# A float32 decoder block on one core: where the first feed-forward's early steps are formed, and in which order its entry runs

## The chip, the cores and the metric

The kernel runs on one core of one Trainium2 chip. The metric is the device time of one execution in microseconds (us); lower is better. The engines are named as in the profile: PE is TensorE (PEld its weight loads), DVE is VectorE, ACT is ScalarE, POOL is GpSimd, SP is SyncE, which only issues DMAs here. "L504" is line 504 of the kernel before.

## The reference, cut to what matters

One layer on 512 tokens of width 1024, all in float32:

```python
h = h + 0.5 * swiglu(rmsnorm(h, ffn1_norm[i]), ffn1_w_gate[i], ffn1_w_up[i], ffn1_w_down[i])
n = rmsnorm(h, mix_norm[i])
...                                     # token mixing: spatial gating beside a state-space part
h = h + jnp.concatenate([ya, yb], axis=-1) @ w_out[i]
h = h + 0.5 * swiglu(rmsnorm(h, ffn2_norm[i]), ffn2_w_gate[i], ffn2_w_up[i], ffn2_w_down[i])
gate = jax.nn.sigmoid(rmsnorm(h, ple_norm[i]) @ ple_w_gate[i] + ple_b_gate[i])
h = h + gate * (p[i] @ ple_w_proj[i])
return rmsnorm(h, final_norm)
```

`p` has 256 features a token. `p @ ple_w_proj`, the embedding product, is used last but depends on nothing else.

## The kernel before, in words

**Precision.** Each float32 operand is split in two: a high part (a cast by ACT, tiles `whi`, `ghi`, `xfa`, `xfb`) and a low part (operand minus high part, mostly by DVE, tiles `wlo`, `glo`, and the second halves of `xfa` and `xfb`). A product is three matmul passes: high by high, high weight by low input, low weight by high input. A weight block is 128x1024 floats (512 KB); its cast is L500, its low part L504.

**The entry.** TensorE first runs ten matmuls on zeros (L181). Then comes the embedding product, in two steps (`embedding(q)`, q = 0 and 1) of four output blocks with 24 matmuls each, since it needs only `p` (256 KB for each half of its features, tile `g`) and a weight block `raw<-in_ple_proj`. Its results wait in DRAM (`emb_dram`) until the end of the kernel; they are copied out of PSUM by L1007 into tiles `embt`, `p7`, `u2` and `rawd`, and stored from there by L967.

Behind it stand four steps on the first group of the first feed-forward (24 matmuls of 512 columns each): gate and up on the first half of the input blocks (`xfa`), then gate and up on the second half (`xfb`). They are plain products. From the second group on the kernel uses a scheme with seven products in place of eight (24 matmuls of 256 columns each, L709), whose inputs are the blocks themselves and their sums and differences. Product number 5 of the scheme takes as its input the difference of the token halves of the first input blocks: `Early.t1` forms it at L614, ScalarE casts it at L617, and GpSimd forms the low part at L620. The differences lie in a tile that takes turns with `embt` in one buffer. The other differences are formed at L648 and L650, cast at L631, their low parts at L634.

The norm's factor is not applied to the inputs but to the products: `RowNorm` sums the squares of the input rows (L361, in the tiles `whix`, `wlox`, `g` and `s1`, which later hold other things), DVE computes the factor with small operations (L233 to L238), spreads it on a diagonal (L297 to L301, tile `tmp`), and two matmuls (L314) on PE bring it to all partitions. They stand on PE between the last of the four plain steps and the first product of the scheme. Scheme product 3 needs a weight block plus another: GpSimd issues a DMA (L761) that adds the second onto the first in `rawb`. Likewise L724 and L727 for other blocks.

**What sets the order.** On PE, ACT, DVE and SP the order of the instructions is the order in which the program writes them. `run` makes a task of each step's load, split, product and after-work, cut into pieces at each `yield`; the table `ENTRY` says which task goes on by how many pieces at the start, and what it doesn't list follows in the loop's own order. GpSimd's queue follows from the program too.

Of the kernel before, what the change touches and what calls it, by code (L numbers as in the profile page):

```python
# [25 lines left out]
F32 = mybir.dt.float32  # L26
# [3 lines left out]
ALU = mybir.AluOpType  # L30

P = 128
T = 512
NC = T // P
D = 1024
ND = D // P
# [4 lines left out]
HT = T // 2  # L41
# [6 lines left out]
LOADS, MIX_LOADS = 6, 4  # L48

ENTRY = """  # L50
load0 load1 load1.1 load2 load3 load3.1 load4 load5 split0 split1:1 split1.1:2 split1 split1.1
load6 load6.1 product0 split2 split3.1:3 split3.1:1 load7 product1 after0 split3:1 split4.1:1
split3 split4.1:1 split3.1:1 split4.1:2 split3.1:1 split4.1:1 split3.1 split4.1 load8 product2
after1:1 after1 split4 split5.1:1 split4.2:2 split5:1 split4.2:2 split5 split5.1:1 split4.2
load9 product3 split5.1 split5.2 split6.2:1 split5.3 product4 split6 split6.1 split6.2:1
split6.2 product5 after4 after4.1 split7 split7.1 load12 product6 split8 after5 product7 sums9
split10.1:1 after6 split9 load14 product8 after7 split10 split10.1 load15 split14:1 product9
split11 after8 load16 split14 product10 after9 split12:1 after10 split12 load17 product11
after11 split13 split15:1 after10.1 split15 product12 split16:1 after12:1 after+10 after11.1
after11.2 product13 split16 after+11 after12 product14 after13:1 sums18 after13 load21 product15  # L60
split17
"""

BUFS = {
# [26 lines left out]
_COL = {}  # L91
# [8 lines left out]
def layer_kernel(ctx: ExitStack, tc: tile.TileContext, a: dict, out: bass.AP):  # L100
    nc = tc.nc
# [44 lines left out]
    def acc_ps():  # L146
        turns["acc"] += 1
        return bank(f"a{turns['acc'] % 2}", 1)
# [6 lines left out]
    def sm_ps():  # L155
        return bank("sm", 3)
# [3 lines left out]


    vec = sb("vec", (P, NVEC))
    nc.scalar.dma_start(vec, a["vecs"])

    def col(name, i):
        c = _COL[name] + i
# [12 lines left out]
    ps = sm_ps()  # L179
# [399 lines left out]
    class Early:  # L579
# [28 lines left out]
        @staticmethod  # L608
        def t1(both):

            f = sb("embt", (P, 2, 2, HT))
            for n, e in enumerate(both):
                x11, x12 = (e.hg[0].rearrange("p k (s t) -> p s k t", s=2)[:, s] for s in range(2))
                nc.vector.tensor_tensor(f[:, n], x11, x12, ALU.subtract)  # L614
                yield
            for n, e in enumerate(both):
                nc.scalar.copy(e.a[:, 1, 0], f[:, n])  # L617
                yield
            for n, e in enumerate(both):
                nc.gpsimd.tensor_tensor(e.a[:, 1, 1], f[:, n], e.a[:, 1, 0].bitcast(F32), ALU.subtract)  # L620
                yield

        @staticmethod
# [34 lines left out]
    def former(name, xfs):  # L658

        neg = sb(f"neg{name}", (P, ND))  # L660
        nc.vector.tensor_scalar(neg, vec[:, _COL[name] : _COL[name] + ND], -1.0, None, ALU.mult)

        def done(d):
            c = (col(name, d), neg[:, d : d + 1])
            if d < NP:
                XForms(xfs).first(h[d], c)
            else:
                xfs[d - NP].second(h[d], c)
        return done
# [293 lines left out]
    pe, stores = [], []  # L963

    def store_embedding():
        for to, t in stores:
            nc.sync.dma_start(to, t)  # L967

    def embedding(q):
        w = Parts()  # L970
        ps = []
        raw = sb("g", (P, 2, T)) if q == 0 else None

        def load():
            if q:
                w.load(a["ple_proj"][q])
                return
            nc.sync.dma_start(raw[:, 0], a["p"][:, 0])
            w.load(a["ple_proj"][q])
            nc.sync.dma_start(raw[:, 1], a["p"][:, 1])  # L980

        def split():
            if q:
# [11 lines left out]

        def product():

            for i in range(4):
                ps.append(acc_ps() if i == 3 else bank("mm", 3) if q else sm_ps())
                accumulate(ps[i], (w.hi, w.lo), 2 * i, pe)  # L1000

        def out():
            for i, tag in enumerate(("embt", "embt", "p7", "u2", "rawd", "rawd", "rawd", "rawd")[4 * q : 4 * q + 4]):
# [47 lines left out]
    ffn1_steps = steps  # L1051
# [95 lines left out]
    for name in ORDER:  # L1147
        kind, i = name[0], int(name[1]) if name != "dt" else 0
# [235 lines left out]
    n = at["x4"] + 1  # L1384
# [82 lines left out]
    n = at["z0"]  # L1467
    for j in range(ND):
        n = at[f"z{j}"]
# [5 lines left out]
    n = at["z0"] + 2  # L1475
# [100 lines left out]
    n = at["v7"]  # L1576
# [7 lines left out]
    for j in range(ND):  # L1584
        n = at[f"z{j}"]
# [220 lines left out]
def _laid_out(i):  # L1806
# [88 lines left out]
```

## Time and profile before

| | before |
|---|---|
| median of 3 runs | 1083.53 us (1083.05 to 1084.03) |
| the profiled execution | 1082.95 us, span 1081.2 us |
| PE, DVE, ACT, POOL busy | 1069.3, 780.3, 515.6, 139.4 us |
| granted TensorE clock, mean | 0.998 |
| DMA moved | 163.77 MB, mean 151 GB/s |

The span is the time from the first to the last instruction; 1.75 us of the profiled execution lie around it. TensorE is busy for 99% of the span, so a change can gain only what TensorE waits for, and most of that lies in the first 43 us and in the last few. In the rows of the timeline the columns are start, duration, engine, line, operation, tiles, shape, and in brackets the idle time before it with what ended it. A busy matmul's duration overlaps the next one's; the pace is the distance between starts.

### The profile page before, as it was taken

How to read it: one execution, taken by the hardware profiler on the slowest of the kernel's cores; microseconds unless marked ns; L12 is line 12 of the kernel's file. 1: busy time of each engine (PE TensorE's matmuls, PEld its weight loads, DVE VectorE, ACT ScalarE, POOL GpSimd, SP SyncE). 2: the span in 40 equal slices, each digit the busy share in tenths (PEclk: the TensorE clock that was granted, in tenths of full speed). 3: DMA queues.
4: the chain of work that ended last, by engine and by line, in shares of the span. 5: the costliest groups of instructions: out<-in, count | busy, mean ns of one | idle time of the engine just before them, and what ended most of it. 6: DMA issues, size and time to landing. Idle time of an engine off the chain costs nothing.

```text
span 1081.2 us, 16536 instructions
## 1 busy us (share of the span) xinstructions
PE 1069.3 (99%) x6679; PEld 946.3 (88%) x6679; DVE 780.3 (72%) x1078; ACT 515.6 (48%) x711; POOL 139.4 (13%) x127
## 2 busy tenths in 40 slices
PE   9999999999999999999999999999999999999997
PEld 7899999999998788787878888899999999999886
DVE  7887776766666686766997656778766676667766
ACT  7644343434444455575654434354444444343554
POOL 0200000000000300143233000000000000000411
PEclk9999999999999999999999999999999999999999
DMA  9987766575523332444332333667756676633412
GB/s 362 274 223 195 196 177 190 150 193 169 137 59 117 98 98 81 137 137 137 125 109 79 98 98 98 214 160 201 220 140 161 190 193 178 177 116 106 145 42 79
DMA packets 49741, 163.77 MB, mean 151 GB/s; under 512 B 5632, under 2 KB 5888, under 8 KB 49664
## 3 DMA queue, kind: packets, MB, share of 16 engines
q1 hardware_dynamic: 39584, 128.99, 35.1%
q0 software_dynamic: 8640, 31.46, 16.9%
q10 hardware_dynamic: 1440, 2.26, 0.7%
q8 instruction: 52, 0.85, 0.3%
q14 instruction: 25, 0.20, 0.1%
HBM read 158.43 MB, written 4.26 MB: 150 GB/s over the span
## 4 chain that ended last, share of the span: by engine, by line
PE 88%; DVE 6%; DMA 3%; ACT 2%; issue 1%; DVEq 0%; SPq 0%; ACTq 0%
PE mm L709 20%; PE a L709 15%; PE sm L216 10%; PE sm L215 10%; PE sm L217 10%; PE mm L216 4%; PE mm L215 4%; PE mm L217 4%; PE a L215 3%; PE a L217 3%; PE a L216 3%; DMA emb_dram<-embt 1%; DVE wlo L504 1%; DMA whix<-in_x_rows 1%; DMA raw<-in_ffn_gu 1%
## 5 line engine op out<-in xcount | busy, mean ns | idle before, releaser
L500 ACT CAST whi<-raw 128x1024 fp32r<-128x1024 f32 x138 | 144.3, 1046 | 159.8 <-issue 56.8
L504 DVE TENSOR_TENSOR wlo<-raw,whi 128x1024 fp32r<-128x1024 f32 x137 | 171.9, 1255 | 61.6 <-ACT whi L500 60.0
L709 PE MATMUL mm<-xfb,whi 128*128 128x256 f32 x960 | 166.0, 276 | 0.0
L709 PEld LDWEIGHTS mm<-xfb,whi 128*128 128x128 f32 x960 | 145.8, 188 | 1.6
L709 PE MATMUL mm<-xfb,wlo 128*128 128x256 f32 x480 | 132.6, 276 | 0.0
L217 PE MATMUL sm<-ghi,wlox 128*128 128x512 f32 x296 | 116.3, 393 | 0.0
L216 PE MATMUL sm<-glo,whix 128*128 128x512 f32 x296 | 115.9, 391 | 0.0
L215 PE MATMUL sm<-ghi,whix 128*128 128x512 f32 x296 | 115.1, 389 | 0.0
L709 PE MATMUL a<-xfb,whi 128*128 128x256 f32 x640 | 110.9, 276 | 0.0
L709 PEld LDWEIGHTS a<-xfb,whi 128*128 128x128 f32 x640 | 97.8, 188 | 1.9 <-issue 0.2
L709 PEld LDWEIGHTS mm<-xfb,wlo 128*128 128x128 f32 x480 | 90.1, 188 | 0.0
L709 PE MATMUL a<-xfb,wlo 128*128 128x256 f32 x320 | 88.4, 276 | 0.4 <-DVE wlo L504 0.4
L504 DVE TENSOR_TENSOR wlox<-rawd,whix 128x1024 fp32r<-128x1024 f32 (+1 forms) x40 | 45.6, 1141 | 58.8 <-ACT whix L500 58.8
L504 DVE TENSOR_TENSOR wlo<-rawb,whi 128x1024 fp32r<-128x1024 f32 x52 | 64.7, 1244 | 19.9 <-ACT whi L500 19.8
L852 ACT ACTIVATE g<-g 128x512 f32<-128x512 f32 x40 | 25.3, 632 | 106.3 <-DVE g L850 106.3
L724 POOL DMA_DIRECT2D raw<-in_ffn_gu x20 | 17.3, 865 | 404.1 <-DMA raw<-in_ffn_gu 120.9
L908 DVE SCALAR_TENSOR_TENSOR h<-sm,h 128x512 f32<-128x512 f32 x96 | 63.2, 683 | 6.4 <-PE sm L217 5.8
L500 ACT CAST whi<-rawb 128x1024 fp32r<-128x1024 f32 x52 | 54.3, 1044 | 28.4 <-DVE rawb L719 17.7
L217 PEld LDWEIGHTS sm<-ghi,wlox 128*128 128x128 f32 x296 | 55.5, 188 | 11.7
L215 PEld LDWEIGHTS sm<-ghi,whix 128*128 128x128 f32 x296 | 55.6, 188 | 10.8
L216 PEld LDWEIGHTS sm<-glo,whix 128*128 128x128 f32 x296 | 55.5, 188 | 10.8
L709 PEld LDWEIGHTS a<-xfb,wlo 128*128 128x128 f32 x320 | 60.1, 188 | 0.6 <-DVE wlo L504 0.6
(417 smaller groups left out, 2497.1 us busy)
## 6 DMA issues: line engine op xcount, KB each, us to landing
raw<-in_ffn_gu SPq DMA_DIRECT2D x56, 512.0 KB, 5.9
rawd<-in_ffn_down SPq DMA_DIRECT2D x40, 512.0 KB, 4.0
rawb<-in_ffn_gu SPq DMA_DIRECT2D x32, 512.0 KB, 5.3
raw<-in_ffn_gu POOLq DMA_DIRECT2D x30, 512.0 KB, 5.6
raw<-in_w_in SPq DMA_DIRECT2D x29, 512.0 KB, 3.6
s<-in_ffn_gu SPq DMA_DIRECT2D x20, 512.0 KB, 6.8
s<-in_ffn_gu POOLq DMA_DIRECT2D x20, 512.0 KB, 8.3
raw<-in_w_out SPq DMA_DIRECT2D x16, 512.0 KB, 3.6
```

Of the source, the lines that this page charges most:

```text
L215: nc.tensor.matmul(ps, whi, xhi, start=first, stop=False)
L216: nc.tensor.matmul(ps, whi, xlo, start=False, stop=False)
L217: nc.tensor.matmul(ps, wlo, xhi, start=False, stop=last)
L500: nc.scalar.copy(self.hi[:, : self.n], self.raw[:, : self.n])
L504: nc.vector.tensor_tensor(self.lo[:, :n], self.raw[:, :n], self.hi[:, :n].bitcast(F32), ALU.subtract)
L709: nc.tensor.matmul(o, wt[:, c], xt, start=fresh and p == m == n == 0, stop=last and n == 2, skip_group_check=True,)
L724: nc.gpsimd.dma_start(w21.raw, self.src[0], accum_op=ALU.add)
L852: nc.scalar.activation(t, t, AF.Silu)
L908: nc.vector.scalar_tensor_tensor(h[d], ps[d], 0.5, h[d], ALU.mult, ALU.add)
```

## The change

Five edits.

1. The embedding product goes by input block: for each half of `p`'s features all four output banks take high by high, then high weight by low input, then low weight by high input. The host lays the weight out to match, so that the first half of the input features has the first half of the columns, and the weight of step q = 0 is loaded in two DMAs of 256 KB.
2. The vector of norm gains (`vec`) is loaded by SP, behind these loads, and no longer by ACT's queue.
3. `Early.t1` puts its differences in the buffer `whix`, and its low parts are formed by VectorE.
4. The negated gains of the second feed-forward (`neg`) are formed in the last step of the first feed-forward.
5. The table `ENTRY` is written anew. `store_embedding` empties its list as it goes; it issues the same five stores.

```diff
 ENTRY = """
-load0 load1 load1.1 load2 load3 load3.1 load4 load5 split0 split1:1 split1.1:2 split1 split1.1
...
+load0 load1 load1.1 load2 load3 load3.1 split0 load4 split1:1 load5 split1.1:2 split1 split1.1
...
     vec = sb("vec", (P, NVEC))
-    nc.scalar.dma_start(vec, a["vecs"])
...
         def t1(both):
 
-            f = sb("embt", (P, 2, 2, HT))
+            f = sb("whix", (P, 2, 2, HT))
...
             for n, e in enumerate(both):
-                nc.gpsimd.tensor_tensor(e.a[:, 1, 1], f[:, n], e.a[:, 1, 0].bitcast(F32), ALU.subtract)
+                nc.vector.tensor_tensor(e.a[:, 1, 1], f[:, n], e.a[:, 1, 0].bitcast(F32), ALU.subtract)
                 yield
...
         neg = sb(f"neg{name}", (P, ND))
-        nc.vector.tensor_scalar(neg, vec[:, _COL[name] : _COL[name] + ND], -1.0, None, ALU.mult)
+        also(
+            ffn1_steps[-1], "split",
+            lambda: nc.vector.tensor_scalar(
+                neg, vec[:, _COL[name] : _COL[name] + ND], -1.0, None, ALU.mult
+            ),
+        )
...
     def store_embedding():
-        for to, t in stores:
-            nc.sync.dma_start(to, t)
+        while stores:
+            nc.sync.dma_start(*stores.pop(0))
...
             nc.sync.dma_start(raw[:, 0], a["p"][:, 0])
-            w.load(a["ple_proj"][q])
+            w.raw = sb(w.tag, (P, 1024))
+            for k in range(2):
+                c = slice(k * T, (k + 1) * T)
+                nc.sync.dma_start(w.raw[:, c], a["ple_proj"][q][:, c])
             nc.sync.dma_start(raw[:, 1], a["p"][:, 1])
+            nc.sync.dma_start(vec, a["vecs"])
...
         def product():
 
-            for i in range(4):
-                ps.append(acc_ps() if i == 3 else bank("mm", 3) if q else sm_ps())
-                accumulate(ps[i], (w.hi, w.lo), 2 * i, pe)
+            ps.extend(acc_ps() if i == 3 else bank("mm", 3) if q else sm_ps() for i in range(4))
+            for k, (xhi, xlo) in enumerate(pe):
+                for n, (wt, xt) in enumerate(((w.hi, xhi), (w.hi, xlo), (w.lo, xhi))):
+                    for i in range(4):
+                        c = slice((4 * k + i) * P, (4 * k + i + 1) * P)
+                        nc.tensor.matmul(ps[i], wt[:, c], xt, start=k == n == 0, stop=k == 1 and n == 2)
...
-    o["ple_proj"] = np.ascontiguousarray(pj.transpose(0, 2, 1, 3).reshape(2, P, 8 * P))
+    o["ple_proj"] = np.ascontiguousarray(
+        pj.reshape(2, 4, P, 2, P).transpose(0, 2, 3, 1, 4).reshape(2, P, 8 * P)
+    )
```

What this does to the queues, at three places.

On PE, before, the first step of the embedding product finishes one bank after the other (`sm_188`, `sm_195`, ... are PSUM banks; `ghi`, `glo` are the parts of `p`, `whi`, `wlo` those of the weight):

```order
L215 MATMUL sm_188<-ghi_152,whi_154 128x512
L216 MATMUL sm_188<-glo_153,whi_154 128x512
L217 MATMUL sm_188<-ghi_152,wlo_155 128x512
L215 MATMUL sm_195<-ghi_152,whi_154 128x512
L216 MATMUL sm_195<-glo_153,whi_154 128x512
L217 MATMUL sm_195<-ghi_152,wlo_155 128x512
```

Now it begins with twelve matmuls on the first input half, four banks in turn for each kind of part:

```order
L1010 MATMUL sm_188<-ghi_148,whi_150 128x512
L1010 MATMUL sm_189<-ghi_148,whi_150 128x512
L1010 MATMUL sm_190<-ghi_148,whi_150 128x512
L1010 MATMUL a_59_191<-ghi_148,whi_150 128x512
L1010 MATMUL sm_188<-glo_149,whi_150 128x512
L1010 MATMUL sm_189<-glo_149,whi_150 128x512
L1010 MATMUL sm_190<-glo_149,whi_150 128x512
L1010 MATMUL a_59_191<-glo_149,whi_150 128x512
L1010 MATMUL sm_188<-ghi_148,wlo_151 128x512
L1010 MATMUL sm_189<-ghi_148,wlo_151 128x512
L1010 MATMUL sm_190<-ghi_148,wlo_151 128x512
L1010 MATMUL a_59_191<-ghi_148,wlo_151 128x512
```

The parts of the second input half are first read by the thirteenth matmul, where before they were read by the fourth. The rest of PE's order, up to the end of the kernel, is as before.

On DVE, before, the two differences of `Early.t1` (`embt_370`) stand on both sides of the low parts for scheme products 4 (`xfb`) and 1 (`wlo_401`), ahead of the norm's small operations (`nv`, ...):

```order
L650 SCALAR_TENSOR_TENSOR glo_275<-glo_223,glo_275 128x512
L614 TENSOR_TENSOR embt_370<-ghi_167 128x512
L634 TENSOR_TENSOR xfb_110<-ghi_272,xfb_110 128x512
L634 TENSOR_TENSOR xfb_112<-glo_275,xfb_112 128x512
L504 TENSOR_TENSOR wlo_401<-rawb_178,whi_400 128x1024
L614 TENSOR_TENSOR embt_370<-ghi_171 128x512
L233 TENSOR_SCALAR nv_435<-rtok_323 128x4
```

Now the differences come earlier (`whix_328`), and the norm's small operations follow the last formed difference of the other kind at once:

```order
L612 TENSOR_TENSOR whix_328<-ghi_167 128x512
L632 TENSOR_TENSOR xfb_111<-glo_277,xfb_111 128x512
L612 TENSOR_TENSOR whix_328<-ghi_171 128x512
L502 TENSOR_TENSOR wlo_364<-rawb_165,whi_363 128x1024
L648 SCALAR_TENSOR_TENSOR ghi_275<-glo_267,ghi_275 128x512
L648 SCALAR_TENSOR_TENSOR glo_277<-glo_270,glo_277 128x512
L231 TENSOR_SCALAR nv_375<-rtok_367 128x4
```

The low parts of `Early.t1` (`xfa<-whix`), new on DVE, follow the two diagonals:

```order
L502 TENSOR_TENSOR wlo_418<-rawb_178,whi_417 128x1024
L295 CAST tokp_421<-rtok_374 128x4
L296 TENSOR_TENSOR tokp_422<-rtok_374,tokp_421 128x4
L299 TENSOR_TENSOR tmp_425<-ident_71,tokp_421 128x512
L299 TENSOR_TENSOR tmp_427<-ident_71,tokp_422 128x512
L618 TENSOR_TENSOR xfa_108<-whix_328,xfa_108 128x512
L618 TENSOR_TENSOR xfa_110<-whix_328,xfa_110 128x512
L502 TENSOR_TENSOR wlo_461<-raw_220,whi_460 128x1024
```

Up to the second diagonal DVE has the same operations as before, in another order, without the `neg` at its start.

On POOL, before, the two low parts stand between the DMAs that add one weight block to another, and the addition into `rawb_178` (for scheme product 3) is behind those into `raw_609` and `s_126`:

```order
L724 DMA raw_226<-in_ffn_gu 128x1024
L727 DMA s_65_229<-in_ffn_gu 128x1024
L620 TENSOR_TENSOR xfa_109<-embt_370,xfa_109 128x512
L620 TENSOR_TENSOR xfa_111<-embt_370,xfa_111 128x512
L724 DMA raw_609<-in_ffn_gu 128x1024
L727 DMA s_126_612<-in_ffn_gu 128x1024
L761 DMA rawb_178<-in_ffn_gu 128x1024
```

Now the two are gone, and the addition into `rawb_178` comes first:

```order
L727 DMA raw_220<-in_ffn_gu 128x1024
L730 DMA s_63_223<-in_ffn_gu 128x1024
L764 DMA rawb_178<-in_ffn_gu 128x1024
L727 DMA raw_610<-in_ffn_gu 128x1024
L730 DMA s_126_613<-in_ffn_gu 128x1024
```

More of the change, by code (lines that the diff above doesn't have):

```diff
@@ L50 @@
 ENTRY = """
-load0 load1 load1.1 load2 load3 load3.1 load4 load5 split0 split1:1 split1.1:2 split1 split1.1
[L52 to L61, printed above, removed]
+load0 load1 load1.1 load2 load3 load3.1 split0 load4 split1:1 load5 split1.1:2 split1 split1.1
+load6 load6.1 product0 split2 load7 product1 after0 split3 split3.1:6 split4.1:3 split4.2:1
+split4.1:1 split4.2:1 split3.1 load8 product2 split4.2:1 after1 split4 split4.1 split4.2:1
+split4.2:1 split6.2:1 split4.2 load9 split6.2:1 product3 split5 split5.1 split6.1 split5.2
+after4:1 split5.3 product4 split6 after4 split6.2 product5 after4.1 split7 split7.1 load12
+product6 split8:1 after5:1 split8 sums9 after6 after5:2 split9:1 split10:1 split10.1:1 after5
+product7 split9 load14 product8 after7 split10 split10.1 split14:1 load15 product9 split11
+after8 split14 load16 product10 after9 after10 split12 load17 after10.1:1 product11 after11
+split13 after10.1 product12 after+10 after11.1:1 after12:1 after11.1 after11.2 product13
+after+11 split15 after12 product14 after13:1 split16 after13
 """
```

## The prediction

> **What bounds the kernel now.** The page comes first. PE is busy for 1069.3 of 1081.2 us, so I look only for what PE waits for.
>
> ```profile
> span 1081.2 us, 16536 instructions
> PE 1069.3 (99%) x6679; PEld 946.3 (88%) x6679; DVE 780.3 (72%) x1078; ACT 515.6 (48%) x711; POOL 139.4 (13%) x127
> ```
>
> Second, PE's waits in the first 160 us (engine, line, releaser; us in total, times, longest):
>
> ```profile
> PE sm L314 <- DVE tmp L301: 1.1, 1, 1.1
> PE sm L215 <- ACT whi L992: 0.2, 1, 0.2
> ```
>
> A wait shows as idle time only when the matmul before it has drained, so, third, the distances between starts in PE's timeline:
>
> ```profile
> 4.82 1.42 PE L181 MATMUL sm<-tmp 128*128 128x512 f32 x3
> 5.67 0.56 PE L181 MATMUL sm<-tmp 128*128 128x512 f32 x1
> ...
> 6.43 0.50 PE L215 MATMUL sm<-ghi,whi 128*128 128x512 f32 x1 [0.20 <-ACT whi L992]
> ...
> 7.16 0.50 PE L217 MATMUL sm<-ghi,wlo 128*128 128x512 f32 x1
> ...
> 7.81 0.50 PE L216 MATMUL sm<-glo,whi 128*128 128x512 f32 x1
> 8.15 0.40 PE L217 MATMUL sm<-ghi,wlo 128*128 128x512 f32 x1
> 8.39 0.39 PE L215 MATMUL sm<-ghi,whi 128*128 128x512 f32 x1
> ...
> 12.59 0.39 PE L215 MATMUL mm<-ghi,whi 128*128 128x512 f32 x1
> ...
> 40.34 0.40 PE L217 MATMUL a<-xfb,wlo 128*128 128x512 f32 x1
> 41.81 1.10 PE L314 MATMUL sm<-tmp,onesr 128*128 128x512 f32 x2 [1.07 <-DVE tmp L301]
> 42.75 0.40 PE L709 MATMUL mm<-xfa,whi 128*128 128x256 f32 x2
> ```
>
> The pace is (12.59 - 8.39) / 18 = 0.233 us for a matmul of 512 columns. The matmuls on zeros go at (5.67 - 4.82) / 2 = 0.425, about half of it; the last hands over at 5.67 + 0.425 = 6.10. The first six real matmuls take until 8.39, where six at full pace from 6.10 end at 7.50: **0.89 us lost at the start.** At the norm's factor, PE could go on at 40.34 + 0.23 = 40.57 and needs 2 x 0.233 for the two L314; the scheme begins at 42.75: **1.71 us lost.** In between the starts are 0.23 apart.
>
> Fourth, who is late. At the start (ACT casts, then DVE low parts):
>
> ```profile
> 4.32 0.62 ACT L992 CAST ghi<-g 128x512 fp32r<-128x512 f32 x1 [1.58 <-DMA g<-in_p]
> 5.76 0.62 ACT L992 CAST whi<-raw 128x512 fp32r<-128x512 f32 x1 [0.83 <-DMA raw<-in_ple_proj]
> 6.41 0.62 ACT L992 CAST ghi<-g 128x512 fp32r<-128x512 f32 x1
> 6.94 0.62 ACT L992 CAST whi<-raw 128x512 fp32r<-128x512 f32 x1
> ...
> 6.41 0.69 DVE L993 TENSOR_TENSOR wlo<-raw,whi 128x512 fp32r<-128x512 f32 x1 [0.75 <-ACT whi L992]
> 7.07 0.69 DVE L993 TENSOR_TENSOR glo<-g,ghi 128x512 fp32r<-128x512 f32 x1
> ```
>
> The whole 512 KB of weight must land (5.74) before the first cast; PE takes each part as it comes: `wlo` ends at 7.10 and is used at 7.16, `glo` of the second half ends at 7.76 and is used at 7.81. At the factor it is DVE:
>
> ```profile
> 25.46 1.22 DVE L504 TENSOR_TENSOR wlo<-raw,whi 128x1024 fp32r<-128x1024 f32 x1
> ...
> 30.74 0.69 DVE L650 SCALAR_TENSOR_TENSOR glo<-glo,glo 128x512 f32<-128x512 f32 x1
> 32.91 0.69 DVE L614 TENSOR_TENSOR embt<-ghi 128x512 f32<-128x512 f32 x1 [1.49 <-DMA emb_dram<-embt]
> ...
> 34.73 2.33 DVE L504 TENSOR_TENSOR wlo<-rawb,whi 128x1024 fp32r<-128x1024 f32 x1
> ...
> 38.37 0.16 DVE L238 SCALAR_TENSOR_TENSOR ny<-nt,ny 128x4 f32<-128x4 f32 x1
> 38.57 1.20 DVE L236 TENSOR_TENSOR nt<-ny 128x4 f32<-128x4 f32 x1
> ...
> 41.07 1.29 DVE L301 TENSOR_TENSOR tmp<-ident,tokp 128x512 fp32r<-128x512 f32 x2
> ...
> 34.68 1.30 POOL L620 TENSOR_TENSOR xfa<-embt,xfa 128x512 fp32r<-128x512 f32 x1 [6.01 <-ACT xfa L617]
> 38.45 1.30 POOL L620 TENSOR_TENSOR xfa<-embt,xfa 128x512 fp32r<-128x512 f32 x1 [2.47 <-ACT xfa L617]
> ...
> 21.06 11.83 DMA emb_dram<-embt
> ```
>
> DVE stands for 1.49 us until the store of the embedding results has left `embt`, whose buffer the differences need (the chain's row: 11.83 us). A low part of 1.22 takes 2.33, and a small operation of 0.16 takes 1.20, just while GpSimd runs L620. Together 1.49 + 1.11 + 1.04 = 3.64 us, and the second diagonal, at 42.36, comes 1.79 us after PE is free.
>
> **The change part by part.**
>
> *Embedding product.* The split load brings the first weight half earlier: halfway between the landings behind 4.32 and 5.76, about 5.04 (an estimate from these two rows, since half the bytes lie between). Cast, 0.62: 5.66, before the matmuls on zeros end. So the first real matmul starts at 6.10. Its next needs: low part of `p`, cast 4.94 plus 0.69 makes 5.63, for 7.03; low part of the weight, 5.66 + 0.69 = 6.35, for 7.97. The second input half is, as before, cast by 7.03 and 7.56 and low by 7.76 and (one DVE operation on) 8.4; now it is wanted at 6.10 + 12 x 0.233 = 8.90, 9.83 and 10.76. No wait is left: the second embedding step starts at 6.10 + 24 x 0.233 = 11.70 instead of 12.59. Gain 0.89. Bounds: if the first weight half lands no earlier than the whole does now, the start stays at 6.43 and only the later waits go, 0.56; if everything comes later still, 0.
>
> *The clock.* The first real matmuls go at full pace, those on zeros at half; the switch lies between 5.67 and 6.43. If only at 6.43, the matmuls started from 6.10 on lose half of 0.33, 0.17 us, and the gain is 0.72. The Trainium skill, "TensorE: Matmul & The Clock Gate", Part 1, says that the clock's window runs freely, so that the switch varies by some 500 ns from run to run; by it the first term would be 0.64 to 0.89, and no row here shows a second start to compare.
>
> *Differences in `whix`, low parts on DVE.* The store's wait goes (1.49). The new buffer is free when ACT has squared the row in it, which ACT still does ahead of the differences' turn. With L620 gone from GpSimd the two stretches go (1.11 + 1.04). DVE gains two operations at 0.60 to 0.69, but behind the diagonals. Up to the second diagonal DVE's operations are else the same, so it ends at 42.36 - 3.64 = 38.7, or earlier where the new order also saves its smaller waits. PE gets there at 40.57 - 0.89 = 39.68: a cover of 1 us. Gain 1.71. A new wait of 1.2 us on DVE would cost 0.2 of it.
>
> *What is next late there.* The two new operations delay the low part for scheme product 7:
>
> ```profile
> 42.27 1.22 DVE L504 TENSOR_TENSOR wlo<-raw,whi 128x1024 fp32r<-128x1024 f32 x1
> ...
> 45.70 0.28 PE L709 MATMUL mm<-xfb,wlo 128*128 128x256 f32 x1
> ```
>
> It ends at 38.7 + 2 x 0.69 + 1.22 = 41.3; PE, 2.6 us earlier, wants it at 43.1. Covered.
>
> *`vec`, `neg`, the SP queue.* `vec` goes through SP behind `p`, ahead of `x`; with the split load two issues more stand ahead of the tiles of `x`. The bytes are the same, and the transfers, not the issues, set the landings from 5.74 on. Should the tiles of `x` land later by an issue or two, the two embedding steps on PE hide it: they last until 6.10 + 48 x 0.233 = 17.3, and nothing made from `x` is wanted before. `neg` is one small DVE operation, moved to a stage where DVE has idle time. Nothing each; bounds -0.2 to +0.2.
>
> *PSUM copies.* The tightest cover: gate and up need a bank that ACT has copied out.
>
> ```profile
> 20.90 0.62 ACT L631 CAST xfb<-glo 128x512 fp32r<-128x512 f32 x1 [1.11 <-DVE glo L648]
> ...
> 22.38 1.06 ACT L1007 COPY rawd<-mm 128x512 f32<-128x512 f32 x2
> ...
> 23.78 0.39 PE L215 MATMUL mm<-xfa,whi 128*128 128x512 f32 x1
> ```
>
> PE now wants it at 23.78 - 0.89 = 22.89; the first copy, half of the row, must end by then. Now it ends at 22.38 + 0.53 = 22.91. The new order puts one L631 cast more ahead of it (0.62), and forms both differences before ACT comes to them, which ends waits like the 1.11. With both, 22.4; with the cast alone, 23.5, which would cost 0.6. I take no loss, since the new DVE order has `L648` well ahead, and keep 0.6 as the bound.
>
> **Sum:** 0.89 + 1.71 = 2.60; I take 2.55 for edges. Profiled execution 1082.95 - 2.55 = 1080.4 (span 1078.7); the median, 0.58 above that execution, 1083.53 - 2.55 = **1081.0**. After 43 us PE runs without waits in this trace, and all later work follows PE, so the 2.55 us should stay.
>
> **The rivals.** (0.2%, or 2.17 us, is about what a measurement of this kernel can tell from no change.)
>
> *A, the addition in `rawb` takes it back.* Scheme product 3 has the least in hand:
>
> ```profile
> 49.98 0.85 POOL L761 DMA_DIRECT2D rawb<-in_ffn_gu  x1
> ...
> 58.85 1.05 ACT L500 CAST whi<-rawb 128x1024 fp32r<-128x1024 f32 x1 [3.65 <-DMA rawb<-in_ffn_gu]
> ...
> 59.94 1.23 DVE L504 TENSOR_TENSOR wlo<-rawb,whi 128x1024 fp32r<-128x1024 f32 x1
> ...
> 62.11 0.28 PE L709 MATMUL a<-xfb,wlo 128*128 128x256 f32 x1
> ```
>
> The low part ends at 61.17, used at 62.11: 0.94. If the DMA landed at the same time as now, 2.6 - 0.94 = 1.66 us of the gain would go: 1082.6. Against it: the addition is now first in GpSimd's queue and waits only for the block's earlier use, which comes earlier too. 13%.
>
> *B, ACT is late with the copies*, by the 0.6 us of the bound above, and PE waits ahead of the up step: 1081.6. For it: the cover is thin; against: the 1.11 us. 12%.
>
> *C, slower: four banks in turn.* If changing the PSUM bank at each matmul kept the weight load from hiding, each would cost what 7.81 to 8.15 shows after a wait, 0.34 - 0.23 = 0.10 us. Over 48 matmuls 4.9 us, net 2.3 slower: 1085.8. It decides from 0.054 us a matmul on. Against: between 8.39 and 12.59 the bank changes three times, and the mean stays 0.233. 6%.
>
> *D, slower: the clock falls back.* If the banks in turn left PE idle enough for the half pace, 48 x (0.425 - 0.233) = 9.2 us, net 6.7: 1090.2. The Trainium skill, "TensorE: Matmul & The Clock Gate", "A second HAM failure mode: psum-queue depth-cycling", tells of such a kernel; this trace shows no fall of the pace before the end. 2%.
>
> *E, the change doesn't do it:* DVE is held up elsewhere by as much; only the start gains: 1082.7. 3%.
>
> **How the numbers follow.** My forecast has 64%. Its own range, from the first term's 0.56 and what the edges can give, is 1080.6 to 1081.3. B at 1081.6 and A at 1082.6 belong in the range: 1080.3 to 1082.7; C and D stay out. Faster by over 0.2% (below 1081.36) is the forecast: 0.64; A, B and E lie within it, 0.28; C and D slower, 0.08.
>
> **What would show it.** Right: the second embedding step starts near 11.7 with starts 0.233 apart from 6.1; no idle time ahead of L312, and the scheme begins near 40.2; DVE's differences without a DMA wait, no low part over 1.3 us there. Wrong: starts over 0.3 apart in the first 48 matmuls (C, D); a wait for `rawd<-mm` near 22.9 (B) or for `rawb` near 59 (A).

## The result and the profile after

The changed kernel takes 1081.05 us (median of 16 runs, 1080.69 to 1081.81), the kernel before, beside it, 1083.85 us (16 runs, 1082.29 to 1088.07): ratio 0.9971, 95% interval 0.9963 to 0.9979. The profiled executions are 2.16 us apart (1082.95 and 1080.79), the spans 2.1:

```profile
span 1079.1 us, 16531 instructions
PE 1068.1 (99%) x6679; PEld 946.1 (88%) x6679; DVE 778.9 (72%) x1080; ACT 514.9 (48%) x711; POOL 136.5 (13%) x125
```

PE's waits in the first 160 us of the changed kernel, but for the one ahead of the zeros (engine, line, releaser; total, times, longest): the wait for the diagonals is gone, and one for a PSUM copy has come.

```profile
PE mm L213 <- ACT rawd L1017: 0.5, 1, 0.5
```

PE's timeline after: the first embedding matmuls, the second embedding step, the end of the first gate step, the first of the up step, the two matmuls of the factor, the scheme.

```profile
5.65 0.97 PE L1010 MATMUL sm<-ghi,whi 128*128 128x512 f32 x3
6.45 0.39 PE L1010 MATMUL a<-ghi,whi 128*128 128x512 f32 x1
...
11.35 0.86 PE L1010 MATMUL mm<-ghi,whi 128*128 128x512 f32 x3
...
22.31 0.40 PE L215 MATMUL sm<-xfa,wlo 128*128 128x512 f32 x1
23.20 0.50 PE L213 MATMUL mm<-xfa,whi 128*128 128x512 f32 x1 [0.49 <-ACT rawd L1017]
23.53 0.39 PE L214 MATMUL mm<-xfa,whi 128*128 128x512 f32 x1
...
40.10 0.62 PE L312 MATMUL sm<-tmp,onesr 128*128 128x512 f32 x2
40.55 0.39 PE L712 MATMUL mm<-xfa,whi 128*128 128x256 f32 x2
```

Three stations give the account. The second embedding step starts at 11.35, before at 12.59: 1.24 us gained. Ahead of the up step PE stands from 22.31 + 0.23 = 22.54 until 23.20, and the next start is 0.33 instead of 0.23 later: 0.75 us given back. The scheme begins at 40.55, 0.45 after the first L312, where 1.71 us were lost before: all gained. 1.24 - 0.75 + 1.71 = 2.20, and the scheme begins 42.75 - 40.55 = 2.20 us earlier. From there to the end of the span it is 1038.5 us in both (1081.2 - 42.75 and 1079.1 - 40.55).

DVE after: the differences wait for nothing, and the second diagonal ends at 36.97 + 1.29 = 38.26, well ahead of PE's two matmuls on it, which start at 40.10.

```profile
28.15 0.68 DVE L612 TENSOR_TENSOR whix<-ghi 128x512 f32<-128x512 f32 x1
...
36.97 1.29 DVE L299 TENSOR_TENSOR tmp<-ident,tokp 128x512 fp32r<-128x512 f32 x2
```

ACT tells where the 0.75 comes from. First the kernel before, at the second weight block:

```profile
7.71 1.05 ACT L500 CAST whi<-raw 128x1024 fp32r<-128x1024 f32 x1 [0.15 <-DMA raw<-in_ple_proj]
```

Then the changed kernel:

```profile
3.50 0.62 ACT L999 CAST ghi<-g 128x512 fp32r<-128x512 f32 x1 [1.21 <-DMA g<-in_p]
4.98 0.62 ACT L999 CAST whi<-raw 128x512 fp32r<-128x512 f32 x1 [0.86 <-DMA raw<-in_ple_proj]
...
8.93 1.05 ACT L498 CAST whi<-raw 128x1024 fp32r<-128x1024 f32 x1 [0.87 <-DMA raw<-in_ple_proj]
...
22.57 1.06 ACT L1017 COPY rawd<-mm 128x512 f32<-128x512 f32 x2
```

The first weight half is there at 4.98, but what stands behind it on SP's queue is late: the second weight block by 1.22 us (8.93 against 7.71), and the tiles of `x` are loaded behind it. ACT carries that on, and the first of the two copies ends at 22.57 + 0.53 = 23.10. PE comes 1.24 us earlier, could begin the up step at 22.54, and waits for it.

Scheme product 3, at last: the addition is issued first of its three, and nothing waits. Its low part ends at 57.69 + 1.22 = 58.91 and is used at 59.91.

```profile
47.33 0.84 POOL L764 DMA_DIRECT2D rawb<-in_ffn_gu  x1 [16.84 <-DVE wlo L502]
...
55.99 1.05 ACT L498 CAST whi<-rawb 128x1024 fp32r<-128x1024 f32 x1 [3.20 <-DMA rawb<-in_ffn_gu]
...
57.69 1.22 DVE L502 TENSOR_TENSOR wlo<-rawb,whi 128x1024 fp32r<-128x1024 f32 x1
...
59.91 0.28 PE L712 MATMUL a<-xfb,wlo 128*128 128x256 f32 x1
```

### The profile page after: what moved, and what is told of

Read it like the earlier page. It is cut to its first block, busy times and chain, and to the rows that moved or that the text cites. A ratio compares the mean times of both kernels' runs of the same rounds, so it can differ in the third digit from the quotient of the medians.

```text
span 1079.1 us, 16531 instructions
## 1 busy us (share of the span) xinstructions
PE 1068.1 (99%) x6679; PEld 946.1 (88%) x6679; DVE 778.9 (72%) x1080; ACT 514.9 (48%) x711; POOL 136.5 (13%) x125
## 3 DMA queue, kind: packets, MB, share of 16 engines
q10 hardware_dynamic: 1296, 2.16, 0.6%
## 4 chain that ended last, share of the span: by engine, by line
PE 89%; DVE 5%; ACT 2%; DMA 1%; issue 1%; SPq 1%; DVEq 0%; ACTq 0%
PE mm L712 20%; PE a L712 15%; PE sm L214 10%; PE sm L213 10%; PE sm L215 10%; PE mm L214 4%; PE mm L213 4%; PE mm L215 4%; PE a L213 3%; PE a L215 3%; PE a L214 3%; DVE wlo L502 1%; DVE tmp L1731 1%; DMA raw<-in_w_in 1%; DMA h<-in_x 1%
```

## The experiments

Medians and ranges in us; each ratio is to the kernel before, run beside it. The first four ran together, the second four, and the last four.

| kernel | median (range, runs) | ratio, 95% interval |
|---|---|---|
| differences alone | 1081.28 (1080.93 to 1081.77, 11) | 0.9976, 0.9967 to 0.9985 |
| `vec` on ACT's queue | 1080.84 (1080.26 to 1081.21, 6) | 0.9972, 0.9960 to 0.9983 |
| weight in one load | 1080.75 (1080.44 to 1081.27, 8) | 0.9973, 0.9963 to 0.9984 |
| copies first | 1080.76 (1080.50 to 1081.09, 6) | 0.9969, 0.9958 to 0.9981 |
| buffer alone | 1081.45 (1081.14 to 1082.02, 11) | 0.9975, 0.9966 to 0.9983 |
| VectorE alone | 1082.93 (1082.22 to 1084.53, 11) | 0.9992, 0.9984 to 1.0001 |
| bank by bank | 1082.76 (1081.75 to 1084.29, 11) | 0.9986, 0.9977 to 0.9994 |
| nine zeros | 1080.41 (1080.20 to 1081.32, 6) | 0.9968, 0.9956 to 0.9981 |
| addition last | 1087.18 (1083.87 to 1089.05, 12) | 1.0024, 1.0012 to 1.0035 |
| before, addition first | 1084.07 (1082.84 to 1086.14, 12) | 0.9995, 0.9985 to 1.0006 |
| eight zeros | 1080.85 (1080.42 to 1081.19, 6) | 0.9965, 0.9952 to 0.9978 |
| ten zeros | 1081.30 (1080.79 to 1081.70, 7) | 0.9966, 0.9954 to 0.9979 |

### The factor: the buffer, the engine, or both

**Differences alone**: the kernel before with edit 3 and nothing else.

```diff
-            f = sb("embt", (P, 2, 2, HT))
+            f = sb("whix", (P, 2, 2, HT))
...
-                nc.gpsimd.tensor_tensor(e.a[:, 1, 1], f[:, n], e.a[:, 1, 0].bitcast(F32), ALU.subtract)
+                nc.vector.tensor_tensor(e.a[:, 1, 1], f[:, n], e.a[:, 1, 0].bitcast(F32), ALU.subtract)
```

> The kernel before with edit 3 alone: differences in whix, their low parts on VectorE, the old table, the old embedding product. My theory has two separate terms. This one holds the second alone: DVE no longer waits 1.49 us for the store, nor is it stretched by 1.11 and 1.04, but the two low parts (1.2 us) stand ahead of the norm's operations in the old order, so the second diagonal ends near 42.36 - 3.64 + 1.2 = 39.9, ahead of PE at 40.57: about 1.7 us faster than before, the start as before (first real matmul near 6.4, second embedding step near 12.6). Rival: the new table is needed for it; then PE still waits at the factor, and the time is within 0.5 us of before.

PE's timeline of this kernel:

```profile
12.63 0.40 PE L215 MATMUL mm<-ghi,whi 128*128 128x512 f32 x1
...
41.09 0.40 PE L709 MATMUL mm<-xfa,whi 128*128 128x256 f32 x2
```

The start is that of the kernel before, PE doesn't wait at the factor, and the scheme begins 42.75 - 41.09 = 1.66 us earlier. That is what was expected of it. Most of the whole change's gain is in these two lines; for them the new table isn't needed.

**Buffer alone** and **VectorE alone**: one of the two lines each, the first in the one, the second in the other.

> The kernel before with the differences in whix alone; their low parts stay on GpSimd. It parts the two halves of the factor's term. Of DVE's 3.64 us the store's wait of 1.49 goes, and the first stretch (1.11) should go with it, since the low part of 1.22 us then ends before GpSimd starts; the second stretch, 0.7 to 1.2 us, stays. The second diagonal ends near 40.3 to 40.9 against PE at 40.57: about 1.4 to 1.7 us faster than the profiled run of before. Theory on the spread: runs of the kernel before reach from 1082.3 to 1088, those of the changed one from 1080.7 to 1081.8, because the landing of the store varies and DVE waits for it; then this kernel's runs lie within 1 us, and its median is some 2.3 us below that of before. Rival: GpSimd's part makes the spread; then the runs still lie 3 us apart.

> The kernel before with the low parts on VectorE alone; the differences stay in the buffer that waits for the store. DVE saves the two stretches (2.15 us) and has 1.2 us more ahead of the diagonals: they end near 41.4 in a run in which the store lands as in the profile of before, 0.8 us after PE; 0.9 us faster than before. Theory on the spread: it stays, 3 us between runs, since the store's landing still decides. Rival: the spread goes with GpSimd's part.

With the buffer alone GpSimd still forms the low parts, and DVE's small operations beside it are still stretched. GpSimd, DVE and PE of that kernel:

```profile
34.85 2.70 POOL L620 TENSOR_TENSOR xfa<-whix,xfa 128x512 fp32r<-128x512 f32 x2 [4.80 <-ACT xfa L617]
...
35.05 1.28 DVE L233 TENSOR_SCALAR nv<-rtok 128x4 f32<-128x4 f32 x1
36.37 1.22 DVE L234 TENSOR_SCALAR ny<-nv 128x4 int32<-128x4 int32 x1
...
39.68 1.29 DVE L301 TENSOR_TENSOR tmp<-ident,tokp 128x512 fp32r<-128x512 f32 x2
...
41.36 0.40 PE L709 MATMUL mm<-xfa,whi 128*128 128x256 f32 x2
```

One stretch was expected to go with the store's wait; two are still there, only on other operations. Yet the second diagonal ends at 40.97, late by little, and the gain is nearly all there (0.9975; in the profile the scheme begins 42.75 - 41.36 = 1.39 us earlier): without the store's wait there is room for the stretches. The runs lie within 0.9 us, as expected. With VectorE alone the store's wait stays. The scheme begins at 41.97, 0.78 us earlier than before, but a second wait appears behind it, and the expected 0.9 us don't come (0.9992). DVE, then POOL, ACT and PE of that kernel:

```profile
32.84 0.69 DVE L614 TENSOR_TENSOR embt<-ghi 128x512 f32<-128x512 f32 x1 [1.61 <-DMA emb_dram<-embt]
...
50.84 0.86 POOL L727 DMA_DIRECT2D s<-in_ffn_gu  x1 [0.40 <-issue]
51.38 1.20 POOL L761 DMA_DIRECT2D rawb<-in_ffn_gu  x1
...
61.06 1.05 ACT L500 CAST whi<-rawb 128x1024 fp32r<-128x1024 f32 x1 [6.43 <-DMA rawb<-in_ffn_gu]
...
61.50 0.40 PE L217 MATMUL sm<-ghi,wlo 128*128 128x512 f32 x1
62.16 0.50 PE L709 MATMUL a<-xfb,whi 128*128 128x256 f32 x2 [0.26 <-ACT whi L500]
63.42 0.38 PE L709 MATMUL a<-xfb,wlo 128*128 128x256 f32 x1 [0.76 <-DVE wlo L504]
```

Here the addition into `rawb` is issued last of three, at 51.38, is cast at 61.06, when it has landed, and PE loses 0.43 + 0.92 = 1.35 us at product 3. That is the mechanism of rival A, in a kernel that has half of edit 3 and the old place of the addition.

### The addition's place in GpSimd's queue

**Addition last**: the changed kernel with the addition moved behind the next group's two. GpSimd's instructions are put in the program's order, and the last piece of the step that issues the addition is run later.

```diff
-product7 split9 load14 product8 after7 split10 split10.1 split14:1 load15 product9 split11
-after8 split14 load16 product10 after9 after10 split12 load17 after10.1:1 product11 after11
+product7 split9:1 load14 product8 after7 split10 split10.1 split14:1 load15 product9 split11
+after8 split14 load16 split9 product10 after9 after10 split12 load17 after10.1:1 product11 after11
```

> The changed kernel, with one thing moved: GpSimd issues the first group's addition into rawb last of its three additions (behind raw and s of the next group), where the changed kernel issues it first. Theory (the place in GpSimd's queue decides): the addition can only be issued after the s addition's start at about 52.5, not at 47.3, so it lands some 3 to 5 us later than 55.99; the low part for scheme product 3, which has 1.0 us in hand, comes late, and PE waits there for 1 to 3 us near 60: median 1082 to 1084, with a spread of over 2 us between runs, as in the kernel before. Rival (the wait in the kernel with VectorE alone came from its later differences, not from the queue): no wait near 60, median 1081.0, spread about 1 us.

GpSimd, ACT and PE of this kernel, then busy time and granted clock (the column behind POOL's) by stretches:

```profile
52.76 1.20 POOL L764 DMA_DIRECT2D rawb<-in_ffn_gu  x1
...
63.77 1.04 ACT L498 CAST whi<-rawb 128x1024 fp32r<-128x1024 f32 x1 [10.67 <-DMA rawb<-in_ffn_gu]
...
59.75 0.40 PE L215 MATMUL sm<-ghi,wlo 128*128 128x512 f32 x1
64.86 0.80 PE L712 MATMUL a<-xfb,whi 128*128 128x256 f32 x2 [4.72 <-ACT whi L498]
66.12 0.58 PE L712 MATMUL a<-xfb,wlo 128*128 128x256 f32 x1 [0.47 <-DVE wlo L502]
```

```profile
62.00:62.50 0.50, 0.00 (x0) 0.00 (x0) 0.00 (x0) 0.00 (x0) 0.00 (x0) 1.00 1.03 270
62.50:63.00 0.50, 0.00 (x0) 0.00 (x0) 0.00 (x0) 0.00 (x0) 0.00 (x0) 0.61 1.04 377
...
67.00:69.00 2.00, 2.00 (x11) 2.00 (x11) 2.00 (x5) 1.69 (x3) 0.00 (x0) 0.50 0.41 166
```

The addition is issued 5.43 us later than in the changed kernel (52.76 against 47.33) and ACT's cast comes 7.78 later (63.77 against 55.99). The theory's mechanism holds; its price was too small (1087.18 where 1082 to 1084 was expected), since in the idle time of 4.7 us the granted clock falls to 0.50, stays there beyond 69, and PE pays for the wait a second time. The whole loss in this profile is 7.5 us: from the scheme's begin at 40.84 to the end of the span it is 1086.9 - 40.84 = 1046.1 us, against 1038.5. The changed kernel so depends on the place of one DMA in a queue that no line of the diff names. The Trainium skill, "TensorE: Matmul & The Clock Gate", Part 1, says that the clock falls to half after an idle window of some 3.4 us: the trace shows the fall, and none after the 2.16 us of the run bank by bank below, but it comes sooner than by the page: the last matmul ends at 59.75 + 0.40 = 60.15, and the clock falls between 62.50 and 63.00 (at 62.61 in the trace's record of the clock), some 2.5 us into the idle time.

**Before, addition first**: the kernel before, GpSimd put in the program's order, which places the addition ahead of the other two. The other engines' queues are the same.

```diff
         mybir.EngineType.PE, mybir.EngineType.Activation, mybir.EngineType.DVE, mybir.EngineType.SP,
+        mybir.EngineType.Pool,
```

> The kernel before, with only GpSimd's queue altered: in each group the addition into rawb is issued ahead of the next group's two additions; all other engines have the same instructions in the same order. Theory (the kernel before has two clusters, near 1083.5 and 1085.7, because the addition stands last and sometimes lands after product 3 wants it): the upper cluster goes, the spread falls from about 4 us to 1.5, and the median is 1082.5 to 1083.2, some 1 us below that of the kernel before. Rival (the spread comes from the wait for the store of the embedding results, or from the start): two clusters as before, median 1083.5 to 1084.3.

The rival holds: 0.9995, and the range of the runs is still 3.3 us, in two groups. So the place of the addition isn't what makes the runs of the kernel before range so widely. Its DVE still waits for the store of `embt`:

```profile
32.58 0.69 DVE L614 TENSOR_TENSOR embt<-ghi 128x512 f32<-128x512 f32 x1 [0.93 <-DMA emb_dram<-embt]
```

### The start: order of the product, loads, copies

**Bank by bank**: the changed kernel with the loops of the embedding product in the old order.

```diff
-            for k, (xhi, xlo) in enumerate(pe):
-                for n, (wt, xt) in enumerate(((w.hi, xhi), (w.hi, xlo), (w.lo, xhi))):
-                    for i in range(4):
+            for i in range(4):
+                for k, (xhi, xlo) in enumerate(pe):
+                    for n, (wt, xt) in enumerate(((w.hi, xhi), (w.hi, xlo), (w.lo, xhi))):
```

> The changed kernel with its product written bank by bank again, on the new weight layout and the split load: the fourth matmul needs the second halves of p and of the weight. Theory: the order by input block is what hides the second half. Here PE waits for ghi (near 7.6), glo (8.25) and wlo (8.9), and the second embedding step starts near 13.1 instead of 11.4 to 12.1: 1.0 to 1.6 us slower than the changed kernel; the wait for the PSUM copies falls away behind it, which gives back up to 0.6. Rival: the order is worth nothing, since the clock holds the first matmuls at half pace anyway: within 0.3 us.

```profile
6.13 0.50 PE L1010 MATMUL sm<-ghi,wlo 128*128 128x512 f32 x1
8.79 0.50 PE L1010 MATMUL sm<-ghi,whi 128*128 128x512 f32 x1 [2.16 <-ACT whi L999]
...
14.14 0.39 PE L1010 MATMUL mm<-ghi,whi 128*128 128x512 f32 x1
```

After three matmuls PE wants the second half and stands for 2.16 us, and the second embedding step starts at 14.14, where 13.1 was expected. The ratio is 0.0015 above the changed kernel's, some 1.6 us. Given the split load, it is the order by input block that hides the second half.

**Weight in one load**: the changed kernel, the first weight block in one DMA.

```diff
-            w.raw = sb(w.tag, (P, 1024))
-            for k in range(2):
-                c = slice(k * T, (k + 1) * T)
-                nc.sync.dma_start(w.raw[:, c], a["ple_proj"][q][:, c])
+            w.load(a["ple_proj"][q])
```

> The changed kernel with the first weight block in one DMA of 512 KB, all else kept. In the kernel before, 512 KB landed 1.45 us behind p; in the changed kernel each half of 256 KB takes 1.25 to 1.5. Theory: the split load costs what it saves; the whole block lands near 5.0, when the first half lands now, the second half of p and x land 1.2 us earlier, and the wait for ScalarE's copies (0.65 us) goes: 0.5 to 0.7 us faster than the changed kernel. Rival, and the step of my prediction: the halves share the time of one load; the whole block lands near 6.2, the first real matmul starts near 6.85, and the time is 1.0 to 1.3 us slower.

ACT, PE, and ACT's copy ahead of the up step:

```profile
3.97 0.62 ACT L996 CAST ghi<-g 128x512 fp32r<-128x512 f32 x1 [1.68 <-DMA g<-in_p]
5.38 0.62 ACT L996 CAST whi<-raw 128x512 fp32r<-128x512 f32 x1 [0.79 <-DMA raw<-in_ple_proj]
...
6.09 0.76 PE L1007 MATMUL sm<-ghi,whi 128*128 128x512 f32 x1
...
22.09 1.06 ACT L1014 COPY rawd<-mm 128x512 f32<-128x512 f32 x2
```

The whole block is there at 5.38 and cast by 6.00; in the changed kernel the half of it is there at 4.98 and cast by 5.60. In this profile the zeros go at half pace to their end, and 6.00 is soon enough for the first real matmul at 6.09. In the changed kernel's own profile the zeros were done by 5.65, and the whole block, landing as here, would have come some 0.35 us late (an estimate from these rows). The times don't tell the two apart (0.9973 and 0.9971): neither the theory's gain of 0.5 to 0.7 us nor the rival's loss of 1.0 to 1.3 came, and these runs don't show the split load to be worth anything.

**`vec` on ACT's queue**: edit 2 undone. **Copies first**: one cast (the piece `split4.2:1`) goes behind the PSUM copies of `after1`.

```diff
+    nc.scalar.dma_start(vec, a["vecs"])
...
-            nc.sync.dma_start(vec, a["vecs"])
```

```diff
-split4.1:1 split4.2:1 split3.1 load8 product2 split4.2:1 after1 split4 split4.1 split4.2:1
+split4.1:1 split4.2:1 split3.1 load8 product2 after1 split4.2:1 split4 split4.1 split4.2:1
```

> The changed kernel with the load of vec back in ScalarE's queue at the start. In the changed kernel p lands at 3.47 instead of 4.29, and x about 1 us later than before; PE then waits 0.65 us for ScalarE's PSUM copies ahead of the up step. Theory one: vec beside p is what delayed p (p back near 4.2, first real matmul past 6.2), and x is late through the split weight load, so x stays late: 0.4 to 0.8 us slower than the changed kernel. Rival: vec's 720-byte rows ahead of x are what makes x late; then x lands 0.6 us earlier and most of the 0.65 us wait goes: the same time as the changed kernel or up to 0.3 us faster.

> The changed kernel with one piece of the table moved: ScalarE copies the two PSUM banks ahead of one cast of a difference (0.53 us) instead of behind it. Theory: PE's wait of 0.65 us ahead of the up step is bound by ScalarE's order, and falls to about 0.1: 0.5 us faster than the changed kernel. Rival: what is late there is x, and another wait takes its place (the same cast, now later, holds DVE or a later product): within 0.2 us of the changed kernel.

Neither has the wait of 0.5 us ahead of the up step. In both PE comes there later than in the changed kernel's profile, as the rows of `vec` on ACT's queue (ACT, then PE) and then of copies first (PE) show:

```profile
21.90 1.06 ACT L1017 COPY rawd<-mm 128x512 f32<-128x512 f32 x2
...
23.33 0.40 PE L214 MATMUL mm<-xfa,whi 128*128 128x512 f32 x1
```

```profile
23.20 0.39 PE L213 MATMUL mm<-xfa,whi 128*128 128x512 f32 x1
```

The up step begins at 23.20 to 23.33 in all three: an early start ends in the wait for the copy, a later one has no wait. The ratios (0.9972, 0.9969, 0.9971) do not tell them apart: the theories' 0.4 to 0.8 us slower and 0.5 faster didn't come, and the times are those of the rivals.

The kernel with `vec` on ACT's queue and the one with a single load also show what made ACT late. SP issues the second weight block at 2.19 in the kernel before, at 3.13 in the changed kernel, and at 2.66 in the kernels with `vec` on ACT's queue and with one load, which have one of the two extra DMAs each. ACT casts it at 7.71, 8.93, 8.42 and 8.60. Each DMA ahead of it so costs part of the 1.22 us; the six other profiles with the changed kernel's loads have the cast still later, at 9.01 to 9.48.

**Nine**, **eight** and **ten zeros**: copies first with `WARM = 9`, 8 and 10 matmuls on zeros ahead of the entry.

> The changed kernel with the PSUM copies ahead of the cast, as in e4, and nine matmuls on zeros instead of ten. In e4 the first real matmul starts at 6.09, when the ten have ended, and runs at half pace until the clock switches (5.1 to 7.1 in the profiles so far). Theory: with the weight half cast near 5.6 the first real matmul starts at 5.67, and a real matmul at half pace takes the place of one on zeros: 0.2 to 0.4 us faster than e4 (1080.4). Rival: the switch comes later by as much as PE's work starts, or the data is not there: no difference, or slower by up to 0.3.

> The changed kernel with the PSUM copies ahead of a cast (as in the run with the copies first) and eight matmuls on zeros instead of ten. If the first weight half is cast in time (about 5.3 to 5.6), each zero less lets a real matmul run in its place at half pace and saves one at full pace: 0.2 us each, so 0.4 below the run with ten zeros beside it, about 1080.3. Rival: the first half is not there, PE idles from 5.25 until 5.6, and it is no better than nine: 0.2 below, about 1080.5. Second rival: the gap in PE's work puts off the switch to full pace, and it is slower than with ten.

> The run with the copies first once more (ten matmuls on zeros), as the measure for eight zeros on the same chip: 1080.7 to 1080.8, ratio to the kernel before about 0.997.

PE with eight zeros, then with ten:

```profile
5.62 1.65 PE L1010 MATMUL sm<-ghi,whi 128*128 128x512 f32 x3 [0.17 <-ACT whi L999]
...
12.23 0.86 PE L1010 MATMUL mm<-ghi,whi 128*128 128x512 f32 x3
```

```profile
6.10 1.48 PE L1010 MATMUL sm<-ghi,whi 128*128 128x512 f32 x3
7.38 0.53 PE L1010 MATMUL a<-ghi,whi 128*128 128x512 f32 x1
...
12.42 0.62 PE L1010 MATMUL mm<-ghi,whi 128*128 128x512 f32 x2
```

With eight the weight isn't there when the zeros end, and the second step starts 0.19 us earlier than with ten, as the rival has it, and not 0.4. The times decide nothing: the medians differ by 0.45 us (1080.85 and 1081.30; nine zeros 1080.41 in another session), the ratios by 0.0001 to 0.0003, within their intervals. In the record of the granted clock the full pace begins at 7.63 with eight and 7.65 with ten, so nothing here speaks for a gap that puts it off; but as that moment moves by 3.3 us between profiles, one profile of each can't show it. Ten zeros are the kernel with the copies first once more: 1081.30, where 1080.7 to 1080.8 was expected, at the expected ratio.

## Why the prediction was right, and where its sizes were not

**Sum and total.** Forecast 1081.0, measured 1081.05; gain by the profiled executions 2.16, forecast 2.55. That the median was met so closely is luck, since two errors cancel: the gain is 0.39 too large, and the median lies 0.26 above the profiled execution after (1081.05 - 1080.79), where 0.58 was carried over from before. That PE runs without waits after 43 us was read from a list that ends at 160 us, and is wrong: over the whole span PE waits there for 0.2 + 0.7 + 0.4 + 0.7 = 2.0 us before and for 0.7 + 0.3 + 0.7 = 1.7 us after. It did no harm: from the scheme's begin to the end it is 1038.5 us in both.

**The factor term, 1.71: right**, shown by the profile after and by differences alone (scheme 1.66 us earlier with the old start). Of its three parts the store's wait carries nearly all: the buffer alone, with both stretches left, gives 0.9975, differences alone 0.9976. The forecast for the second diagonal, 38.7 or earlier, came out as 38.26, and low part 7 made no wait.

**The start term, 0.89: mis-sized.** In its own profile the second step starts at 11.35 (forecast 11.70). But there the full pace began before the first real matmul's turn (at 5.06 in the record of the granted clock; that matmul starts at 5.65, three at (6.45 - 5.65) / 3 = 0.27). In the kernel with the copies first and ten zeros, run again, it began at 7.65: three starts at (7.38 - 6.10) / 3 = 0.427. By the timelines the second step starts in the new order and with ten zeros at 11.35 (after), 11.90 (addition last), 12.01 and 12.42 (copies first), 12.07 (one load) and 12.14 (`vec` on ACT's queue), on the average 11.98; in the old order at 12.39 (VectorE alone), 12.59 (before), 12.63 (differences alone), 12.76 (buffer alone) and 12.81 (before, addition first), on the average 12.64. The term is 0.66 by these single profiles, inside its bounds of 0.56 and 0.89. The step that failed is "the first real matmuls go at full pace": one profile showed it, and the moment moves from run to run by more than the 0.33 us that the bound of 0.72 allowed. The clock isn't all: in addition last the full pace began at 4.59, yet the first real matmul waits 0.24 us for its weight (5.80), and the thirteenth, at 8.47 + 0.23 = 8.70, until 9.00 for the cast of the second half. So "no wait is left" depends on the landings too.

**"The transfers, not the issues, set the landings": not so here**, and so the nothing charged to SP's queue was too little: the second weight block was issued 0.94 us later and cast 1.22 us later, and ACT's first work on `x` stood behind it (9.88, before 8.66). With one of the two extra DMAs taken out it was issued 0.47 us later and cast 0.71 or 0.89 later. The two embedding steps on PE didn't hide it, since ACT's copies came behind it.

**Rival B came, at its place and price** (forecast a wait near 22.9 of 0.6; seen 23.20 and 0.75). It took back what the early clock gave beyond the usual. The forecast named the cast ahead of the copies; the lateness of ACT by the loads came to it, and it took both. Without the cast (0.52 to the next start) the first copy would have ended at 23.10 - 0.52 = 22.58; with the cast, but one of the extra DMAs less, it ended at 21.90 + 0.53 = 22.43 and 22.09 + 0.53 = 22.62. PE wanted it at 22.54. No run has PE at that moment and one of the two causes alone.

**Rival A** didn't come in the changed kernel: the low part has 59.91 - 58.91 = 1.0 us in hand, as its argument had it (the addition first in the queue). VectorE alone and addition last show that the argument was the right one. The price, 1.66, is near the 1.35 of the one and far below the 7.5 of the other, where the clock falls. **C** and **D** didn't come: between 6.45 and 11.35 lie 21 matmuls, 4.90 / 21 = 0.233 each, with the bank changing at each.

**Open:** why the runs of the kernel before range over 5.8 us and those of the changed kernel over 1.1, which adds to the gain by medians. The record narrows it. Of the twelve runs of before with the addition first, the seven up to 1084.38 us all have a mean granted clock of 0.998, the five from 1085.16 on all 0.996; bank by bank has 0.997 to 0.998 in the seven up to 1082.77 and 0.996 to 0.997 in the four from 1083.82 on. Of 1083 us, 0.002 are 2.2 us, about the distance of the groups. So the slower runs seem to have some 4 us more at half pace, as addition last has in its profile; where in the kernel, no trace shows. VectorE alone is of another kind: its slower four have 0.998 to 0.999. The profiles of before and of before with the addition first, whose DVE waits for the store until 32.91 and 32.58, are of runs at the lower end of their ranges; none of a run at the upper end was taken. That of VectorE alone is of one (1084.43), and there it is the addition. The kernels fall in two groups: where PE's time hangs on a DMA that lands just in time (the store of `embt` in before, VectorE alone, and before with addition first; the second half in bank by bank; addition last) the runs range over 2.3 us or more; in the other nine over 1.1 or less. That the landings make the range is likely by this, and not shown.

The lowest ratios to the kernel before are those with the copies first and eight, ten and nine zeros (0.9965, 0.9966, 0.9968); they can't be told from the changed kernel's 0.9971.

## What to carry to other kernels

Before an engine is relieved, look for the tile that makes it wait: a buffer shared with a slow store cost more here than two low parts on the wrong engine, and one line removed it. When work moves earlier, follow every transfer behind it, since in the profile 0.75 of the 1.24 us gained at the start were lost again at the next copy; and where a queue's order follows from the program, look up where the one urgent DMA stands in it. A clock state that one profile shows in its first microseconds is a sample, not a price.

## What the runs showed of the hardware

- The step from half to full pace in TensorE's record of the granted clock (it lies in the traces; the views print only its mean over a stretch) lay between 4.59 and 7.87 us from the span's start over the fourteen profiles of these kernels, though all begin with the same matmuls on zeros at 1.66 or 1.67. The stretches at full pace are 58.03 and 1013.76 us long in addition last, 1071.79 in before, VectorE alone and bank by bank, and 1068.37 in the other ten, and the one at half pace in the middle of addition last 6.83: 17, 297, 314, 313 and 2 times 3.413 us. In these records the clock so changes only on a grid of 3.413 us, and where the grid lies differs from run to run. The Trainium skill, "TensorE: Matmul & The Clock Gate", Part 1, gives a freely running window of some 3.4 us and a variation of some 500 ns either way; the traces agree with the window, and show a variation of 3.3 us in all, about the window's length.
- After 4.7 us without work PE goes on at half pace for 4.6 us (from 64.86 until 69.44 in the record): of the 7.5 us that this wait cost, 5.2 are waits (4.72 + 0.47), most of the rest is the pace.
- Half of the first weight block (256 KB) was there at 4.61 to 5.13 in the eight profiles with the split load, the whole (512 KB) at 5.38 with `vec` on SP and at 5.58 to 5.92 with `vec` on ACT's queue. Against the one profile with a single load the half so came 0.25 to 0.77 us earlier, and with `vec` on SP the next block was cast at 8.93 to 9.48, against 8.60 with one load.
- A DVE operation on four elements a partition takes 1.28 us (35.05 with the buffer alone) beside a GpSimd operation with two inputs, and 0.16 without one (the same operation with differences alone, at 36.37).
